# Value projection of a two-layer decoder trunk by seven block products instead of eight row-tile products, with the residual's affine moved

## The chip, the cores and the metric

The kernel runs on one core of one Trainium2 chip. A core has five engines that run side by side, each through its own queue in order: TensorE (PE in the profile; PEld is its weight load) multiplies matrices, VectorE (DVE) and ScalarE (ACT) work element by element, GpSimd (POOL) does small arithmetic and issues accumulating transfers, and SyncE (SP) issues plain transfers. Operands lie in SBUF with 128 partitions; matmul results land in the eight banks of PSUM, from which VectorE and ScalarE fetch them. The metric is device time in microseconds, the median of several executions. A profile is of one execution, and its span runs from the first to the last instruction.

## The reference

A sequence of 512 tokens with width 1024 passes two layers, all in float32. The first has gated linear attention, the second stick-breaking attention whose keys and values come from one shared projection of the first layer's output. Each layer ends with a squared-ReLU MLP, and after each half stands a residual sum with a layer norm.

```python
kv = h @ kv_w                      # (512, 1024) @ (1024, 2048): keys, then values
q = h @ sb_w_q[j]
o = stick_breaking_attention(q, k_sh, v_sh)
mix = o @ sb_w_o[j]
h = layer_norm(ALPHA * h + mix, ln_g[l, 0], ln_b[l, 0])
h = layer_norm(ALPHA * h + square(relu(h @ w_up)) @ w_down, ln_g[l, 1], ln_b[l, 1])
```

The change concerns the values, `h @ kv_w[:, 1024:]`, a product of 512 x 1024 by 1024 x 1024, and the affine (gain and bias) of the layer norm ahead of it.

## The kernel before

**Float32 by parts.** Each operand of a matmul is split into a high part (`hi`, rounded by a ScalarE copy) and a low part (`lo`, the rest, by a VectorE subtraction). A product is three matmuls, hi x hi, hi x lo and lo x hi (`mm3`, L91). Weights are split in tiles of 128 x 1024 (`split_tile`, L67), with three buffers of raw weights and six each of `hi` and `lo`. `put` (L97) splits anything else the same way.

**Seven products.** The MLP's second matrix is multiplied by Strassen's scheme in Winograd's form (`seven`, L294): tokens, inner dimension and columns are cut in halves, seven products of sums of blocks take the place of eight, and each product is 2 token tiles x 4 slices of 128 x 3 = 24 matmuls. The sums of weight blocks are made by accumulating transfers from GpSimd's queue (`more`) or by VectorE (L373, L383), in tiles tagged `B` with eight buffers. Columns of the second half come out negated, and adds become subtractions. Sums of activation blocks are VectorE operations on tiles of 128 x 1024, which `split_a` (L282) then splits.

**Around the change.** At the end of the first layer's MLP, `done0` (L743) calls `finish` (L245) with the steps that `seven` yields. For each 128-token tile: `stats` and `centre` (VectorE, with two small GpSimd operations between), then `turn`: for each half of the width, four TensorE transposes into a bank, four ScalarE operations that apply gain and bias (now one number per partition) into a scratch tile `y`, and `put` into the split transposed activations `h2T`. `y` is thrown away. Tiles 0 and 1 are turned within `seven`; tiles 2 and 3 come back as a list `late`.

Then (L767 to L773) the values are made plainly: for each half of the columns, four pairs of raw weight blocks are split, and for each token tile `rows` (L263) makes 24 matmuls of 512 columns into a bank, which ScalarE copies into `vs`. The two late turns stand behind the first two row tiles.

Attention follows in eight pairs of heads (L866 to L896). In step p: the key and query projections of pair p+2 with the transposes of pair p's weights between, scores and stick-breaking weights of pair p+1 (VectorE scans, L833, and products with them on GpSimd or, for the last, VectorE, L834), and outputs of pair p. In steps 1 to 4 the residual rows of one token tile get their gain and bias (`affine`, L192: four VectorE operations of 128 x 512).

**What sets the order.** The program's text is not the order of the queues. A planner simulates the engines and gives each engine, whenever it is free, the ready instruction that comes first in the program; `tc.high_priority()` raises some (the statistics and centring). So a later instruction that is ready fills a wait. `tc.keep_in_program_order` pins an instruction behind the one traced last on its engine. Buffers are handed out as they come free. The pool of the attention stage (`sb`) is opened when the MLP's has been closed, and takes its place in SBUF.

Of the kernel before, what the change touches and what calls it, by code (L numbers as in the profile page):

```python
# [8 lines left out]
F32 = mybir.dt.float32  # L9
F32R = mybir.dt.float32r  # L10
I32 = mybir.dt.int32
AF = mybir.ActivationFunctionType
# [22 lines left out]
def yoco_kernel(ctx: ExitStack, tc: tile.TileContext, x, gla_w_in, gla_w_a2, gla_b_a, gla_norm_g,  # L35
# [22 lines left out]
    def unit(dtype):  # L58
        return big.tile([P, 4, 512], dtype, tag="T", bufs=8, name=nm("T"))
# [166 lines left out]
    def turn_affine(sp, u, t, src, cols, y):  # L226

        g, b = cols
        ps = bank()
        for i in range(4):  # L230
            nc.tensor.transpose(out=ps[:, 128 * i:128 * i + 128], in_=src[:, 128 * i:128 * i + 128], identity=ident)  # L231
        for i in range(4):
            k, c = 4 * u + i, slice(128 * i, 128 * i + 128)
            nc.scalar.activation(y[:, c], ps[:, c], AF.Identity, bias=b[:, k:k + 1], scale=g[:, k:k + 1])
        c = slice(128 * t, 128 * t + 128)
        put(sp.hi[u][:, :, c], sp.lo[u][:, :, c], y.rearrange("p (a b) -> p a b", a=4))

    def by_tiles(mm):
        for t in range(NT):
# [2 lines left out]
            if t > 0:  # L242
                yield ~(t - 1)

    def finish(steps, cols, hs, sp, work):  # L245

        def turn(t, work):
            for u in range(2):  # L250
                turn_affine(sp, u, t, hs[t].h[:, 512 * u:512 * u + 512], cols, work())

        rest = list(range(NT))
        for t in steps:
            if t < 0:
                turn(~t, work)
                rest.remove(~t)
            else:
                hs[t].stats()
                hs[t].centre()  # L260
        return [lambda work, t=t: turn(t, work) for t in rest]
# [426 lines left out]
    def mlp(l, hT, late, vec, done):  # L688
# [45 lines left out]
        last, begun = up(NG - 1, lambda: ahead(sq[NG - 2]))  # L734
        sq.append(last)
        steps = down(NG - 2, begun=begun, norms=range(NT) if l == 0 else (2, 3), ends=True)
        got = done(steps, work)
        ml.__exit__(None, None, None)
        return got

    h2T = Split(0)

    def done0(steps, work):  # L743
        h2T.grow()
        h2T.grow()
        return finish(steps, lncols(0, 1), hs, h2T, work)

    late = mlp(0, hT, late, vec, done0)


    sbx = tc.tile_pool(name="sb", bufs=1, reuse_waits="tile")
# [11 lines left out]

    def chain():
        return sbp.tile([P, S], F32, tag="w", bufs=6, name=nm("w"))

    vs = [unit(F32), unit(F32)]  # L767
    for n in range(2):
        pcs = pieces_512(kv_w, 0, 8, D + 512 * n)
        for t in range(NT):  # L770
            nc.scalar.activation(vs[n][:, t, :], rows(h2T, t, pcs, K8), AF.Copy)
            if late:
                late.pop(0)(chain)  # L773

    HALVES = ((A0, A1), (A1, A0))

# [99 lines left out]
    for p in range(NP):  # L876
        if p + 2 < NP:
            pairs[p + 2].keys()
            made = pairs[p].turn()
            pairs[p + 2].queries(lambda k: [next(made, None) for _ in range(TAKE.get(k, 0))])  # L880
        else:
            n = p - (NP - 2)
            pcs = pieces_512(sb_w_o[0], 0, 4, 512 * n)
            made = pairs[p].turn()
            for t in range(NT):
                hs[t].add(n, rows(oA, t, pcs, range(4)), True)
                for _ in range(((0, 1, 2, 2), (1, 1, 2, 1))[n][t]):
                    next(made, None)
        if p + 1 < NP:
            pairs[p + 1].weights()  # L890
        if 1 <= p <= NT:
            hs[p - 1].affine(vec)
        if p in (4, 6):
            u = unit(F32R)
            parts += [(u[:, i, :], u[:, 2 + i, :]) for i in range(2)]
        pairs[p].outputs(*parts[p], LAST if p == NP - 1 else [(j, j, NT) for j in range(NT)])  # L896
# [13 lines left out]
    late = finish(by_tiles(part2), vcols, hs, h3T, chain)  # L910
    sbx.__exit__(None, None, None)

    def done1(steps, work):
        vec = lnvec(1, 1)


# [68 lines left out]
```

## Time and profile before

| | us |
|---|---|
| median of 3 runs (lowest to highest) | 1119.79 (1119.24 to 1119.84) |
| profiled execution, span | 1118.1 |
| median of the runs less this span | 1.7 |
| TensorE busy | 1110.7 |
| VectorE busy | 803.2 |
| ScalarE busy | 551.1 |
| GpSimd busy | 171.3 |

In the rows below, a number and L are a line of the kernel, `x` a count of instructions, an arrow goes from what is read to what is written, and a bracket at the end gives idle time ahead of an instruction and what ended it. In rows of the timeline the first number is the start in us from the span's start and the second the duration. Matmuls overlap in a pipeline, so their rate is read from starts or from long stretches, not from one row's duration.

### The profile page before, as it was taken

The numbers are of one execution on the slowest core, as the hardware profiler recorded it, in microseconds if no ns is written. First come the engines' busy times: TensorE is split into PE (matmuls) and PEld (weight loads), VectorE is DVE, ScalarE is ACT, GpSimd is POOL, SyncE is SP. The second block draws the span as 40 slices with busy tenths as digits, with TensorE's granted clock in tenths as the row PEclk, the third lists the DMA queues.
The fourth block names the chain that finished last, engine by engine and source line by source line (L and its number), as shares of the span: only waits on it lengthen the run. The fifth ranks groups of instructions, "written<-read, shape, count | busy, mean of one in ns | idle before, by whom it ended". The sixth has DMA issues, their size and how long they took to land.

```text
span 1118.1 us, 14353 instructions
## 1 busy us (share of the span) xinstructions
PE 1110.7 (99%) x5515; PEld 919.9 (82%) x5515; DVE 803.2 (72%) x967; ACT 551.1 (49%) x829; POOL 171.3 (15%) x213
## 2 busy tenths in 40 slices
PE   9999999999999999999999999999999999999997
PEld 7888888898888888888888778778988888888885
DVE  4677639958956856848945888887489767667677
ACT  4455437653533534535734666664445435336363
POOL 1011222200100100122200434330200000000232
PEclk9999999999999999999999999999999999999999
DMA  8441399492670770787344221212947816706783
GB/s 248 121 132 57 112 260 213 117 300 92 190 206 24 200 208 19 203 199 144 113 114 132 57 76 39 76 38 57 287 114 202 245 38 168 228 19 187 175 136 86
DMA packets 105368, 157.52 MB, mean 141 GB/s; under 512 B 12306, under 2 KB 37266, under 8 KB 105300
## 3 DMA queue, kind: packets, MB, share of 16 engines
q1 hardware_dynamic: 86772, 120.43, 33.4%
q0 software_dynamic: 18240, 35.66, 18.7%
q8 instruction: 43, 0.70, 0.2%
q10 hardware_dynamic: 288, 0.52, 0.1%
q14 instruction: 25, 0.20, 0.1%
HBM read 153.45 MB, written 3.15 MB: 140 GB/s over the span
## 4 chain that ended last, share of the span: by engine, by line
PE 98%; DVE 1%; issue 0%; POOL 0%; ACT 0%; POOLq 0%; DVEq 0%; ACTq 0%
PE ps L349 29%; PE ps L93 20%; PE ps L94 20%; PE ps L95 20%; PE ps L857 2%; PE ps L843 2%; PE ps L806 2%; PE ps L231 1%; PE ps L578 0%; DVE lo L72 0%; PE ps L121 0%; PE ps L643 0%; DVE bst L177 0%; DVE h L169 0%; PE ps L445 0%
## 5 line engine op out<-in xcount | busy, mean ns | idle before, releaser
L349 PE MATMUL ps<-hi,T 128*128 128x512 f32 x1008 | 313.2, 390 | 0.1
L93 PE MATMUL ps<-T,hi 128*128 128x512 f32 (+1 forms) x768 | 288.8, 376 | 0.0
L94 PE MATMUL ps<-T,hi 128*128 128x512 f32 (+1 forms) x768 | 285.6, 372 | 0.0
L95 PE MATMUL ps<-T,lo 128*128 128x512 f32 (+1 forms) x768 | 285.5, 372 | 0.0
L72 DVE TENSOR_TENSOR lo<-raw,hi 128x1024 fp32r<-128x1024 f32 x134 | 163.1, 1220 | 131.3 <-ACT hi L70 130.5
L70 ACT ACTIVATE hi<-raw 128x1024 fp32r<-128x1024 f32 x134 | 142.1, 1064 | 178.3 <-PE ps L94 62.4
L349 PEld LDWEIGHTS ps<-hi,T 128*128 128x128 f32 x1008 | 188.9, 188 | 40.0 <-DVE T L99 0.6
L349 PE MATMUL ps<-lo,T 128*128 128x512 f32 x504 | 196.1, 389 | 0.0
L70 ACT ACTIVATE hi<-B 128x1024 fp32r<-128x1024 f32 x108 | 114.1, 1059 | 159.2 <-PE ps L94 104.1
L72 DVE TENSOR_TENSOR lo<-B,hi 128x1024 fp32r<-128x1024 f32 x108 | 130.8, 1220 | 83.3 <-ACT hi L70 83.3
L95 PEld LDWEIGHTS ps<-T,lo 128*128 128x128 f32 x768 | 144.7, 188 | 25.1
L93 PEld LDWEIGHTS ps<-T,hi 128*128 128x128 f32 x768 | 144.7, 188 | 24.6 <-issue 0.9
L94 PEld LDWEIGHTS ps<-T,hi 128*128 128x128 f32 x768 | 144.8, 189 | 23.6
L308 POOL DMA_DIRECT2D B<-in_mlp_w_down_dram x52 | 62.8, 1244 | 542.8 <-DMA B<-in_mlp_w_down_dram 327.0
L349 PEld LDWEIGHTS ps<-lo,T 128*128 128x128 f32 x504 | 94.6, 188 | 19.6
L93 PE MATMUL ps<-hi,T 128*128 128x512 f32 x256 | 102.4, 400 | 0.0
L95 PE MATMUL ps<-hi,T 128*128 128x512 f32 x256 | 100.2, 392 | 0.0
L94 PE MATMUL ps<-lo,T 128*128 128x512 f32 x256 | 100.0, 391 | 0.0
L169 DVE TENSOR_TENSOR h<-h,ps 128x512 f32<-128x512 f32 x110 | 74.7, 680 | 6.9 <-PE ps L95 4.0
L834 POOL TENSOR_TENSOR w<-w,r 128x512 f32<-128x512 f32 x32 | 53.0, 1658 | 133.5 <-DVE r L833 125.7
L833 DVE TENSOR_TENSOR_SCAN r<-r,begin 128x512 f32<-128x512 f32 x40 | 66.2, 1659 | 2.4 <-ACT r L830 2.2
L95 PEld LDWEIGHTS ps<-hi,T 128*128 128x128 f32 x256 | 48.1, 188 | 10.9 <-DVE T L99 0.7
(179 smaller groups left out, 1161.2 us busy)
## 6 DMA issues: line engine op xcount, KB each, us to landing
raw<-in_mlp_w_up_dram SPq DMA_DIRECT2D x64, 512.0 KB, 5.5
B<-in_mlp_w_down_dram SPq DMA_DIRECT2D x64, 512.0 KB, 5.9
B<-in_mlp_w_down_dram POOLq DMA_DIRECT2D x52, 512.0 KB, 7.9
raw<-in_gla_w_in_dram SPq DMA_DIRECT2D x20, 512.0 KB, 3.7
raw<-in_mlp_w_down_dram SPq DMA_DIRECT2D x16, 512.0 KB, 4.4
raw<-in_kv_w_dram SPq DMA_DIRECT2D x16, 512.0 KB, 4.2
B<-in_gla_w_o_dram POOLq DMA_DIRECT2D x14, 512.0 KB, 7.8
B<-in_gla_w_o_dram SPq DMA_DIRECT2D x8, 512.0 KB, 7.7
```

Of the source, the lines that this page charges most:

```text
L70: nc.scalar.activation(hi, raw, AF.Copy)
L72: nc.vector.tensor_tensor(lo, raw, hi.bitcast(F32), op=ALU.subtract)
L93: keep(nc.tensor.matmul(ps, lhsT=a[0], rhs=b[0], start=first, stop=False))
L94: keep(nc.tensor.matmul(ps, lhsT=a[0], rhs=b[1], start=False, stop=False))
L95: keep(nc.tensor.matmul(ps, lhsT=a[1], rhs=b[0], start=False, stop=last))
L169: nc.vector.tensor_tensor(h, h, ps, op=op)
L308: nc.gpsimd.dma_start(out=b.rearrange("p (a b) -> p a b", a=2), in_=weights(k, h, j), accum_op=ALU.add)
L349: nc.tensor.matmul(banks[s], lhsT=a(k, s)[x], rhs=b[k][y], start=opens and (k, x, y) == (0, 0, 0), stop=closes and (k, x, y) == (3, 1, 0), ...
L806: nc.tensor.matmul(zs[b + a][:, at], lhsT=self.q[x][own, P * i:P * i + P], rhs=self.k[y][own, 0:n], start=(x + y == 0), stop=(x == 1), ski ...
L833: nc.vector.tensor_tensor_scan(down, down, begins[kind][:, ::-1], 1.0, op0=ALU.mult, op1=ALU.max)
L834: (nc.vector if kind == 2 else nc.gpsimd).tensor_tensor(w, w, r[:, 1:S + 1], op=ALU.mult)
L843: nc.tensor.transpose(out=ps[:, P * b:P * b + P], in_=w[:, P * b:P * b + P], identity=ident)
```

## The change

The values get a seven-product function of their own, `values`, which `done0` calls inside the MLP's pool. `finish` is handed a place for the turned rows: two tiles of the MLP's pool (`four()`) now keep the float32 `y` of all four token tiles, and the sums of activation blocks (a22, a21, a11, a12) are made from these. Three weight sums come about as follows: B22 + B12 and B12 + B11 by accumulating transfers (`more`), and two on VectorE, in two tiles each. B22 is loaded once more for the sixth product. The first two products (`ys`, `xs`) read `h2T` of the first token half alone, and the late turns stand behind the two token tiles of the first. The plain loop and its late turns go. In the attention steps `affine` is now given `tc.keep_in_program_order`.

```diff
@@ turn_affine
-            nc.scalar.activation(y[:, c], ps[:, c], AF.Identity, bias=b[:, k:k + 1], scale=g[:, k:k + 1])
+            nc.scalar.activation(y[:, i, :], ps[:, c], AF.Identity, bias=b[:, k:k + 1], scale=g[:, k:k + 1])
...
-        put(sp.hi[u][:, :, c], sp.lo[u][:, :, c], y.rearrange("p (a b) -> p a b", a=4))
+        put(sp.hi[u][:, :, c], sp.lo[u][:, :, c], y)
@@ finish
-    def finish(steps, cols, hs, sp, work):
+    def finish(steps, cols, hs, sp, work, room=None):
...
-                turn_affine(sp, u, t, hs[t].h[:, 512 * u:512 * u + 512], cols, work())
+                y = room(u, t) if room else work().rearrange("p (a b) -> p a b", a=4)
+                turn_affine(sp, u, t, hs[t].h[:, 512 * u:512 * u + 512], cols, y)
@@ mlp
-        got = done(steps, work)
+        got = done(steps, work, four, mlp_)
...
+    vs = []
+    def values(y, late, pool):
+        a11, a21, a12, a22 = y[0][:, :, 0:256], y[0][:, :, 256:512], y[1][:, :, 0:256], y[1][:, :, 256:512]
+        whole = lambda u, c0: lambda k, s: tuple(w[u][:, k, c0 + 128 * s:c0 + 128 * s + 128] for w in (h2T.hi, h2T.lo))
...
+        def load(k, j, more=None):
+            got = []
+            for h in range(2):
+                b = pool.tile([P, 1024], F32, tag="B", bufs=8, name=nm("B"))
+                v = b.rearrange("p (a b) -> p a b", a=2)
+                nc.sync.dma_start(out=v, in_=weights(k, h, j))
+                if more:
+                    nc.gpsimd.dma_start(out=v, in_=weights(*more(h)), accum_op=ALU.add)
+                got.append(b)
+            return got
...
+        def fresh(s, banks, i, j):
+            nc.scalar.activation(vs[j][:, 2 * i + s, :], banks[s], AF.Copy, scale=-1.0 if j else 1.0)
+        def add(s, banks, i, j):
+            v = vs[j][:, 2 * i + s, :]
+            tt(v, v, banks[s], op=ALU.subtract if j else ALU.add)
+        ys, xs, ws, zs = ([None, None] for _ in range(4))
+        b11, b21 = load(0, 0), load(1, 0)
+        b22 = load(1, 1, lambda h: (0, h, 1))
+        b12 = load(0, 1, lambda h: (0, h, 0))
+        p1, p2 = pieces(b11), pieces(b21)
+        for s in range(2):
+            part(s, whole(0, 0), p1, ys, True, False)
+            late.pop(0)(None)
+        for h in range(2):
+            tt(b11[h], b22[h], b11[h], op=ALU.add)
+            tt(b21[h], b21[h], b11[h], op=ALU.add)
+        p4 = pieces(b21)
+        vs.extend([unit(F32), unit(F32)])
+        for s in range(2):
+            part(s, whole(1, 0), p2, xs)
+        tt(a22, a22, a21, op=ALU.subtract)
+        p5 = split_a(a22), pieces(b12)
+        for s in range(2):
+            part(s, whole(1, 256), p4, ws)
+        for s in range(2):
+            fresh(s, ys, 0, 0)
+            add(s, xs, 0, 0)
+        tt(a21, a11, a21, op=ALU.subtract)
+        minus(a11, a22, a11)
+        p6 = split_a(a11), pieces(b11)
+        for s in range(2):
+            part(s, *p5, zs, True, False)
+            fresh(s, ws, 1, 0)
+            fresh(s, zs, 1, 1)
+        minus(a12, a12, a11)
+        p3 = split_a(a12), pieces(load(1, 1))
+        for s in range(2):
+            part(s, *p6, ys, False, False)
+            fresh(s, ys, 0, 1)
+        p7 = split_a(a21), pieces(b22)
+        for s in range(2):
+            part(s, *p3, zs, False, True)
+            add(s, zs, 0, 1)
+        for s in range(2):
+            part(s, *p7, ys, False, True)
+            add(s, ys, 1, 1)
+            add(s, ys, 1, 0)
...
-        return finish(steps, lncols(0, 1), hs, h2T, work)
+        y = [four(), four()]
+        late = finish(steps, lncols(0, 1), hs, h2T, work, lambda u, t: y[u][:, :, 128 * t:128 * t + 128])
+        values(y, late, pool)
...
-    vs = [unit(F32), unit(F32)]
-    for n in range(2):
-        pcs = pieces_512(kv_w, 0, 8, D + 512 * n)
-        for t in range(NT):
-            nc.scalar.activation(vs[n][:, t, :], rows(h2T, t, pcs, K8), AF.Copy)
-            if late:
-                late.pop(0)(chain)
...
-            hs[p - 1].affine(vec)
+            hs[p - 1].affine(vec, tc.keep_in_program_order)
```

`part` is the 12 matmuls of one token tile as in `seven`, and `pieces` splits a list of B tiles with `split_tile`. In the text the products are counted in the order in which they stand: `p1`, `p2`, `p4`, `p5`, `p6`, `p3`, `p7`.

More of the change, by code (lines that the diff above doesn't have):

```diff
@@ L741, in yoco_kernel, with pieces, part @@
     h2T = Split(0)
-    def done0(steps, work):
+    vs = []
+    def values(y, late, pool):
+        a11, a21, a12, a22 = y[0][:, :, 0:256], y[0][:, :, 256:512], y[1][:, :, 0:256], y[1][:, :, 256:512]
+        whole = lambda u, c0: lambda k, s: tuple(w[u][:, k, c0 + 128 * s:c0 + 128 * s + 128] for w in (h2T.hi, h2T.lo))
+        weights = lambda k, h, j: block(kv_w, 512 * k + 256 * h, D + 512 * j)
+        tt = nc.vector.tensor_tensor
+        def load(k, j, more=None):
[8 more added lines that the diff above has]
+            return got
+        def pieces(bs):
+            got = []
+            for b in bs:
+                hi, lo = split_tile(b, 2)
+                got += [(hi[:, i, :], lo[:, i, :]) for i in range(2)]
+            return got
+        def part(s, a, b, banks, opens=True, closes=True):
+            if opens:
+                banks[s] = bank()
+            for k in range(4):
+                for x, w in ((0, 0), (0, 1), (1, 0)):
+                    nc.tensor.matmul(banks[s], lhsT=a(k, s)[x], rhs=b[k][w],
+                                     start=opens and (k, x, w) == (0, 0, 0),
+                                     stop=closes and (k, x, w) == (3, 1, 0), skip_group_check=True)
+        def fresh(s, banks, i, j):
[26 more added lines that the diff above has]
+        tt(a21, a11, a21, op=ALU.subtract)
+        minus = lambda out, a, b: nc.vector.scalar_tensor_tensor(out, a, -1.0, b, op0=ALU.mult, op1=ALU.subtract)
+        minus(a11, a22, a11)
[17 more added lines that the diff above has]
+            add(s, ys, 1, 0)
@@ L744, in done0 @@
+    def done0(steps, work, four, pool):
         h2T.grow()
         h2T.grow()
-        return finish(steps, lncols(0, 1), hs, h2T, work)
-    late = mlp(0, hT, late, vec, done0)
+        y = [four(), four()]
+        late = finish(steps, lncols(0, 1), hs, h2T, work, lambda u, t: y[u][:, :, 128 * t:128 * t + 128])
+        values(y, late, pool)
+    mlp(0, hT, late, vec, done0)
     sbx = tc.tile_pool(name="sb", bufs=1, reuse_waits="tile")
@@ L911, in yoco_kernel, with done1 @@
     sbx.__exit__(None, None, None)
-    def done1(steps, work):
+    def done1(steps, work, *_):
         vec = lnvec(1, 1)
```

## The prediction

> **What bounds the kernel now.** I read the page's first and fourth parts, then windows around the stage that is changed, then single rows of each engine there.
>
> ```profile
> PE 1110.7 (99%) x5515; PEld 919.9 (82%) x5515; DVE 803.2 (72%) x967; ACT 551.1 (49%) x829; POOL 171.3 (15%) x213
> ...
> PE 98%; DVE 1%; issue 0%; POOL 0%; ACT 0%; POOLq 0%; DVEq 0%; ACTq 0%
> ```
>
> TensorE (PE) is busy 99% of the span and carries 98% of the chain that ended last. So time is won only where TensorE gets less to do, and only as long as the other engines keep it fed. The chain of waits, in order of time, gives its rate:
>
> ```profile
> 446.11 38.08 PE ps L349 x168
> ...
> 540.57 5.47 PE ps L349 x24
> ...
> 551.48 0.87 PE ps L231 x8
> ```
>
> An earlier pair of `down` groups, seven products of 24 matmuls, took 38.08 us for 168 matmuls: 0.2267 us each (the 0.39 us of a single row overlap). The MLP's last 24 end at 540.57 + 5.47 = 546.0, and there the value projection begins. A turn of one 128-token tile, eight transposes, is 0.87 us. The stage's last eviction:
>
> ```profile
> L771 ACT ACTIVATE T<-ps x8: 598/600/601, 551.5 to 591.4; 128x512 f32<-128x512 f32 x8
> ```
>
> It starts at 591.4. By the rates, 192 x 0.2267 + 2 x 0.87 = 45.3 us after 546.0 is 591.3: TensorE runs through the old stage without a gap. The windows show what room the others have:
>
> ```profile
> 506.00:546.00 40.00, 40.00 (x185) 32.97 (x184) 38.49 (x47) 25.31 (x38) 7.96 (x9) 1.00 0.56 120
> 546.00:559.00 13.00, 13.00 (x68) 10.87 (x67) 12.23 (x20) 8.88 (x18) 4.23 (x11) 1.00 0.51 158
> ...
> 576.00:588.00 12.00, 12.00 (x54) 9.95 (x53) 0.00 (x0) 1.90 (x3) 0.00 (x0) 1.00 0.16 46
> ```
>
> Columns are the stretch, its length, and busy time of PE, PEld, DVE, ACT and POOL, then granted clock (full), DMA share and GB/s. VectorE (DVE) is nearly full at the MLP's end (38.5 of 40 us, 12.2 of 13), and idle from 576 to 588. The change fills this idle stretch, but its first products must get through the full one.
>
> **The change part by part.** *Removed from TensorE:* 8 row tiles x 24 = 192 matmuls become 7 products x 24 = 168. 24 x 0.2267 = **-5.44 us**. The two turns stay. ScalarE's eight evictions stay too (now `fresh`).
>
> *Weights.* Eight splits of raw blocks become fourteen of B tiles. Ten plain loads go on SP in place of eight; four accumulating loads go on GpSimd's queue.
>
> ```profile
> B<-in_mlp_w_down_dram SPq DMA_DIRECT2D x64, 512.0 KB, 5.9
> B<-in_mlp_w_down_dram POOLq DMA_DIRECT2D x52, 512.0 KB, 7.9
> ...
> L308 POOL DMA_DIRECT2D B<-in_mlp_w_down_dram x52 | 62.8, 1244 | 542.8 <-DMA B<-in_mlp_w_down_dram 327.0
> ```
>
> The MLP's last B tiles are split in the 506 to 546 window, so slots come free from about 510 to 533; 5.9 + 7.9 us later, by about 547, the sums are there. I cost them at nothing, because VectorE has other work until then; uncovered, a sum that lands late moves the third product by as much. Each issue holds GpSimd 1.24 us, and the two `pow` of tiles 2 and 3 queue behind: 0 to 2 x 1.24 on a turn, which TensorE bridges with the other half of the first product, as that needs only tiles 0 and 1. 0 taken. The later raw loads of SP queue behind the tenth B load, which waits for a slot; their users start after 585, so 0.
>
> *Added to VectorE*, in the order in which it must come. These are its rows around the start:
>
> ```profile
> 545.52 0.68 DVE L169 TENSOR_TENSOR h<-h,ps 128x512 f32<-128x512 f32 x1
> 546.12 0.68 DVE L196 TENSOR_TENSOR h<-h,lng 128x512 f32<-128x512 f32 x1
> 546.72 0.68 DVE L177 BATCH_NORM_STATS2 bst<-h 128x6 f32<-128x512 f32 x1
> 547.33 0.67 DVE L99 TENSOR_TENSOR T<-s,T 128x512 fp32r<-128x512 f32 x1
> ...
> 548.59 1.21 DVE L72 TENSOR_TENSOR lo<-raw,hi 128x1024 fp32r<-128x1024 f32 x1
> 549.72 0.68 DVE L177 BATCH_NORM_STATS2 bst<-h 128x6 f32<-128x512 f32 x1
> 550.33 0.86 DVE L190 TENSOR_SCALAR h<-h,mv,rs 128x1024 f32<-128x1024 f32 x1
> ...
> 551.22 1.16 DVE L72 TENSOR_TENSOR lo<-raw,hi 128x1024 fp32r<-128x1024 f32 x1
> 553.15 0.81 DVE L190 TENSOR_SCALAR h<-h,mv,rs 128x1024 f32<-128x1024 f32 x1 [0.77 <-POOL rs L184]
> 553.88 1.22 DVE L72 TENSOR_TENSOR lo<-raw,hi 128x1024 fp32r<-128x1024 f32 x1
> ```
>
> From start to start a 128x1024 operation takes 1.13 (548.59 to 549.72) and a 128x512 one 0.60 (545.52 to 546.12). By 553.88 + 1.13 = 555.0 VectorE has done the adds, statistics and centring of tiles 2 and 3, the split at 548.59, one affine operation (546.12) and two more splits (551.22, 553.88), and was idle 0.77. In the new kernel the affine operation is gone and those two splits are not yet due: 0.60 + 2 x 1.13 + 0.77 = 3.6 us of room, which takes three of the four new 128x1024 weight sums. After 555.0 the **third product** (the one with the summed weights on the second token half) still needs: one sum 1.13, the low halves of both turns 4 x 0.60, its first weight split 1.13; together 4.7, so it can start at 559.7 at the earliest (its second split, 1.13, hides behind the 6 x 0.2267 = 1.36 us on the first). TensorE is there at 546.0 + 48 x 0.2267 + 2 x 0.87 = 558.6. The least stall is **1.1**.
>
> The most: VectorE takes what is ready, and the fourth product's weight splits (2 x 1.13) and the two adds of the second product (2 x 0.60) are ready before the chain of sum, ScalarE's copy and low half is; add one such copy for which VectorE waits:
>
> ```profile
> 484.37 2.00 ACT L70 ACTIVATE hi<-B 128x1024 fp32r<-128x1024 f32 x2
> ...
> 552.02 1.85 ACT L234 ACTIVATE w<-ps,bcol,gcol 128x128 f32<-128x128 f32 x5
> ```
>
> One copy is 2.00 / 2 = 1.0, so the most is 1.1 + 2.3 + 1.2 + 1.0 = 5.6. ScalarE is no easier just then: sixteen row-affine pieces at 1.85 / 5 = 0.37 lie ahead of that copy. The old rows show VectorE filling each short wait with whatever was ready (the affine piece at 546.12 between an add and its statistics), which is between the ends; I take **3.0**.
>
> *Fourth to seventh product.* From the third's start VectorE needs for the fourth a difference, its low half and two splits, 4 x 1.13 = 4.5, plus the third's second split 1.13: 5.7 against the 5.44 that the third lasts, with one ScalarE copy (1.0) inside the chain. 0 to 1.5; taken **0.6**. The sixth product's inputs cost 4.5 and the fifth's 5.7; the seventh's, with the two adds before it, 4.6, each against 5.44 of TensorE. Over the whole stage that is some 35 us of VectorE from 545.5 to 580, where TensorE starts the seventh at 580 plus the stalls: it fits, if hardly. Nothing more, bound 1. The last four adds fall into the key projection.
>
> *Residual's affine.* It leaves the value stage:
>
> ```profile
> L196 DVE TENSOR_TENSOR h<-h,lng 128x512 f32<-128x512 f32 x8 | 5.3, 685 | 0.0
> L196 DVE TENSOR_TENSOR h<-h,lnb 128x512 f32<-128x512 f32 x8 | 5.2, 685 | 0.0
> ```
>
> Sixteen operations at 0.60 are 9.6 us. All but the one counted above ran after 555; without the move they would only have filled leftover time, so it relieves nothing beyond that 0.60. Pinned behind the last VectorE operation of each pair's weights, they now come four at a time, 2.4 us, in pairs 1 to 4. A period of that stage:
>
> ```profile
> 665.16 1.23 DVE L72 TENSOR_TENSOR lo<-raw,hi 128x1024 fp32r<-128x1024 f32 x1 [2.44 <-ACT hi L70]
> ...
> 667.92 1.23 DVE L833 TENSOR_TENSOR_SCAN r<-r,begin 128x512 f32<-128x512 f32 x1 [0.20 <-ACT r L830]
> ...
> 669.37 2.12 DVE L833 TENSOR_TENSOR_SCAN r<-r,begin 128x512 f32<-128x512 f32 x1
> ...
> 676.87 1.30 DVE L834 TENSOR_TENSOR w<-w,r 128x512 f32<-128x512 f32 x1
> 678.10 0.68 DVE L99 TENSOR_TENSOR T<-ps,T 128x512 fp32r<-128x512 f32 x1
> 678.70 1.21 DVE L72 TENSOR_TENSOR lo<-raw,hi 128x1024 fp32r<-128x1024 f32 x1
> 679.83 0.68 DVE L99 TENSOR_TENSOR kl<-ps,kh 128x512 fp32r<-128x512 f32 x1
> 682.95 1.23 DVE L72 TENSOR_TENSOR lo<-raw,hi 128x1024 fp32r<-128x1024 f32 x1 [2.44 <-ACT hi L70]
> ```
>
> The period is 682.95 - 665.16 = 17.79, with 2.44 idle before the row at 682.95. The four go in at 678.10; the output's and the key's low halves and one split come 2.41 later, and the gap shrinks to 0.03. So **0**, with work on the path only past that gap: the whole of it uncovered is 4 x 2.41 = 9.6. Two PSUM banks (outputs, keys) are freed 2.4 later; the key's still at 683.0, when the next scores have just begun on other banks.
>
> The sum: -5.44 + 3.0 + 0.6 + 0 = -1.84. The profiled execution spans 1118.1, and the median of the runs is 1119.79, 1.7 around it. 1118.1 - 1.8 = 1116.3 of span, **1118.0** as a time. Its own range goes from -5.44 + 1.1 = -4.3 (1115.4) to -5.44 + 5.6 + 1.5 = +1.7 (1121.4).
>
> **The rivals.** *Full gain.* VectorE's order follows need: the third product waits 1.1 or less, nothing after. 1114.4 to 1115.6. For it: that order wants no more work than the rows show. Against: the rows fill each wait with what is ready, not with what is due.
>
> *Nothing left.* The change does not do what it says because VectorE becomes the bound: every low half comes late, the fourth and later products stall by some 0.5 each as well: -5.44 + 3.0 + 4 x 0.5 + a late sum of 1 is +0.6, 1120.4. For it: 12.23 of 13 us. Against: the idle 576 to 588, which the work can flow into.
>
> *Slower.* In pairs 1 to 4 the inserted operations outgrow the gap. It decides from 0.03 us per pair on, once the low halves of keys and outputs are late by more than scores and turns can wait. A scan beside GpSimd's product took 2.12 (669.37) where the first of a pair takes 1.23 (667.92), so an operation can stretch by 0.9 there; the gap lost in full gives 1118.0 + 9.6 = 1127.6, and four stretches a pair 14 us on top of what the gap hides, 1132. Against: they start at 678.10, when
>
> ```profile
> 675.84 1.79 POOL L834 TENSOR_TENSOR w<-w,r 128x512 f32<-128x512 f32 x1
> ```
>
> GpSimd's last product has ended, at 677.6. The Trainium skill, SBUF — State Buffer, section Who interferes with whom, says that a VectorE instruction with two inputs in SBUF blocks, or is blocked by, a GpSimd instruction that reads SBUF; the affine operations are of this kind, and the row at 669.37 agrees with it. By that rule they must stay behind 677.6, as the pin has them.
>
> **How the numbers follow.** Against no change a measurement here can tell about 0.2%, 2.24 us: faster is below 1117.55, slower above 1122.03. Forecast 0.62, full gain 0.14, nothing left 0.12, slower 0.12. Of the forecast's own range about two fifths lie below 1117.55: 0.14 + 0.26 = 0.40 faster; 0.12 slower and 0.01 for the forecast's upper end, 0.13; the rest, 0.47, the same. The range 1114.9 to 1121.5 leaves out the slower rival and the lowest part of the full gain, 0.05.
>
> **What would show it.** 168 matmuls on a new line at 0.2267; a TensorE gap of 1 to 5.6 us after 48 of them, released by a VectorE low half of a B tile, little or none later; affine operations behind 678 less the gain, with the idle 2.44 gone from four periods and the period still 17.8. Gaps in pairs 1 to 4, or none before the third product, would prove me wrong.

## The result and the profile after

The changed kernel takes **1127.79 us** (median, 1126.49 to 1130.47) against 1119.72 us (1119.24 to 1119.84) for the kernel before; the ratio is 1.0075, with a 95% interval of 1.006 to 1.0089. It is slower. The forecast was 1118.0 with a range up to 1121.5. The profiled execution took 1126.58 us and spans 1124.9, 6.8 more than the 1118.1 before. It is one of the two faster of the four runs, so the trace shows 6.8 of the 8.1 us between the medians; in the two slower runs the mean granted clock was 0.995 and 0.996, in the two faster 0.998.

The first part of the page after, and the group of the new matmuls from the view of groups by line, taken over the value stage alone:

```profile
PE 1109.5 (99%) x5491; PEld 917.6 (82%) x5491; DVE 828.1 (74%) x993; ACT 559.7 (50%) x839; POOL 176.2 (16%) x217
...
L777 PE MATMUL ps<-hi,T 128*128 128x512 f32 x112 | 35.6, 393 | 1.7 <-DVE T L99 1.0 <-ACT T L98 0.7
L777 PE MATMUL ps<-lo,T 128*128 128x512 f32 x56 | 22.0, 392 | 0.0
```

The 24 matmuls are gone (5515 to 5491), 168 stand on the new line, and VectorE has 24.9 us more to do. Three marks on TensorE cut the difference into stages: the first matmul of the values, the first scores and the last scores. Rows of the timeline, the kernel before:

```profile
545.88 0.39 PE L93 MATMUL ps<-hi,T 128*128 128x512 f32 x1
...
607.60 0.50 PE L806 MATMUL ps<-kh,qh 64*128 64x512 f32 x2
...
737.20 0.28 PE L806 MATMUL ps<-kh,ql 64*128 64x256 f32 x2
```

and the kernel after:

```profile
549.96 0.39 PE L777 MATMUL ps<-hi,T 128*128 128x512 f32 x1
...
611.68 0.50 PE L889 MATMUL ps<-kh,qh 64*128 64x512 f32 x2
...
743.50 0.28 PE L889 MATMUL ps<-kh,ql 64*128 64x256 f32 x2
```

| stage | before | after | difference |
|---|---|---|---|
| up to the first value matmul | 545.88 | 549.96 | +4.1 |
| from there to the first scores (values, then key and query of the first pairs) | 61.72 | 61.72 | 0.0 |
| first scores to last scores | 129.60 | 131.82 | +2.2 |
| from there to the end of the span | 380.9 | 381.4 | +0.5 |

So the value stage gained nothing from 24 fewer matmuls, and two neighbours became longer. What made the last 0.5 no run shows.

**Ahead of the values.** GpSimd's queue in the kernel after (L760 issues the accumulating loads of the value weights, L183 and L184 are `ve` and the `pow` of the statistics):

```profile
534.79 3.73 POOL L760 DMA_DIRECT2D B<-in_kv_w_dram  x3 [9.48 <-DVE h L169]
538.07 0.90 POOL L183 TENSOR_SCALAR ve<-mv 128x1 f32<-128x1 f32 x2
540.33 1.22 POOL L760 DMA_DIRECT2D B<-in_kv_w_dram  x1 [1.36 <-DMA B<-in_kv_w_dram]
541.10 1.94 POOL L184 TENSOR_TENSOR rs<-ve,mhalf 128x1 f32<-128x1 f32 x2
```

The same tiles' statistics before:

```profile
535.91 0.22 POOL L183 TENSOR_SCALAR ve<-mv 128x1 f32<-128x1 f32 x1 [13.64 <-DVE mv L182]
536.21 0.57 POOL L184 TENSOR_TENSOR rs<-ve,mhalf 128x1 f32<-128x1 f32 x1
```

The `pow` of tiles 0 and 1 stands behind the fourth accumulating load, which waits until 540.33 for its own plain load to land: 4.9 us late (541.10 against 536.21). The chain of waits of the kernel after, in order of time, shows that this lay on the path (columns: start, length, what):

```profile
531.88 1.07 ACT hi L70
...
534.23 5.54 DMA B<-in_kv_w_dram
539.84 0.49 issue
540.33 1.22 POOL B L760
541.55 0.62 POOL rs L184
542.20 0.82 DVE h L190
543.07 3.35 PE ps L231 x16
...
558.19 0.82 DVE h L190
559.06 1.09 PE ps L231 x8
```

TensorE waits 2.27 us before the turns at 543.07 and then needs 3.35 us for sixteen transposes, where 2 x 0.87 = 1.74 was the old price. The window after this wait:

```profile
543.00:546.00 3.00, 2.93 (x16) 2.93 (x17) 2.94 (x5) 2.10 (x6) 0.04 (x1) 0.58 1.12 204
```

The granted clock was 0.58 there. The chain also shows that the load which `pow` queued behind started only at 534.23, when VectorE had split the MLP's late weight (531.88) and its buffer was free.

At 559.06 a second wait of 2.47 us stands before tile 3's turn, again behind `pow` and centring. Two more follow in the fifth product, at 577.55 and 579.74. From start to start, less 0.2267 for the matmul between, the three cost 2.6, 0.9 and 1.2 us, 4.7 together. The rest is spread out: the last 68 matmuls take 15.70 us from 579.74, 0.231 each in place of 0.2267, which over 168 is 0.7. That makes the 5.4 us that the seven products saved.

**In the pairs.** VectorE in the kernel after, between two scores, and TensorE beside it:

```profile
664.43 1.28 DVE L196 TENSOR_TENSOR h<-h,lng 128x512 f32<-128x512 f32 x2
665.63 1.28 DVE L196 TENSOR_TENSOR h<-h,lnb 128x512 f32<-128x512 f32 x2
666.84 0.68 DVE L99 TENSOR_TENSOR T<-ps,T 128x512 fp32r<-128x512 f32 x1
667.44 1.21 DVE L72 TENSOR_TENSOR lo<-raw,hi 128x1024 fp32r<-128x1024 f32 x1
668.57 0.68 DVE L99 TENSOR_TENSOR kl<-ps,kh 128x512 fp32r<-128x512 f32 x1
...
669.31 0.50 PE L889 MATMUL ps<-kh,qh 64*128 64x512 f32 x1 [0.52 <-DVE kl L99]
```

The scores wait for the key's low half, which the four affine operations pushed back. This happens in two of the four pairs, whose periods are 18.84 and 18.83 us (from 668.29 to 687.13 and from 704.96 to 723.79) where 17.79 was usual.

### The profile page after: what moved, and what is told of

It reads as the page before. It is cut to its first block, busy times and chain, and to the rows that moved or that the text cites. A ratio compares the mean times of both kernels' runs of the same rounds, so it can differ in the third digit from the quotient of the medians.

```text
span 1124.9 us, 14368 instructions
## 1 busy us (share of the span) xinstructions
PE 1109.5 (99%) x5491; PEld 917.6 (82%) x5491; DVE 828.1 (74%) x993; ACT 559.7 (50%) x839; POOL 176.2 (16%) x217
## 4 chain that ended last, share of the span: by engine, by line
PE 88%; DVE 3%; issue 3%; DMA 3%; POOL 1%; ACT 0%; POOLq 0%; DVEq 0%; ACTq 0%
PE ps L350 23%; PE ps L93 18%; PE ps L94 18%; PE ps L95 18%; PE ps L777 3%; DMA B<-in_mlp_w_down_dram 2%; PE ps L940 2%; PE ps L889 2%; PE ps L926 1%; PE ps L231 1%; DVE lo L72 1%; DVE T L99 1%; POOL B L309 1%; DMA B<-in_kv_w_dram 0%; DVE h L169 0%
## 5 line engine op out<-in xcount | busy, mean ns | idle before, releaser
L350 PE MATMUL ps<-hi,T 128*128 128x512 f32 x1008 | 313.6, 390 | 0.1
L72 DVE TENSOR_TENSOR lo<-raw,hi 128x1024 fp32r<-128x1024 f32 x126 | 153.6, 1222 | 105.9 <-ACT hi L70 105.6
L350 PEld LDWEIGHTS ps<-hi,T 128*128 128x128 f32 x1008 | 189.3, 188 | 40.1 <-DVE T L99 0.6
L70 ACT ACTIVATE hi<-raw 128x1024 fp32r<-128x1024 f32 x126 | 133.4, 1062 | 165.7 <-PE ps L94 65.4
L70 ACT ACTIVATE hi<-B 128x1024 fp32r<-128x1024 f32 x122 | 128.4, 1061 | 173.3 <-PE ps L94 105.4
L72 DVE TENSOR_TENSOR lo<-B,hi 128x1024 fp32r<-128x1024 f32 x122 | 147.9, 1222 | 88.1 <-ACT hi L70 88.1
L350 PE MATMUL ps<-lo,T 128*128 128x512 f32 x504 | 196.2, 389 | 0.0
L93 PE MATMUL ps<-hi,T 128*128 128x512 f32 x192 | 77.5, 404 | 0.0
L95 PE MATMUL ps<-hi,T 128*128 128x512 f32 x192 | 75.3, 392 | 0.0
L94 PE MATMUL ps<-lo,T 128*128 128x512 f32 x192 | 75.0, 391 | 0.0
L99 DVE TENSOR_TENSOR T<-s,T 128x1024 fp32r<-128x1024 f32 (+1 forms) x50 | 53.5, 1071 | 6.9 <-ACT T L98 6.9
```

The source lines that it names most:

```text
L70: nc.scalar.activation(hi, raw, AF.Copy)
L72: nc.vector.tensor_tensor(lo, raw, hi.bitcast(F32), op=ALU.subtract)
L93: keep(nc.tensor.matmul(ps, lhsT=a[0], rhs=b[0], start=first, stop=False))
L94: keep(nc.tensor.matmul(ps, lhsT=a[0], rhs=b[1], start=False, stop=False))
L95: keep(nc.tensor.matmul(ps, lhsT=a[1], rhs=b[0], start=False, stop=last))
L99: keep(nc.vector.tensor_tensor(lo, ps, hi.bitcast(F32), op=ALU.subtract))
```

## The experiments

All are compared with runs of the kernel before on the same chip (median 1119.6 to 1120.2). The ratio has an interval of its own and isn't the quotient of two medians: for e10 that would be 1.0020. The three marks are read from the rows as above, and are those of one execution of each kernel; the times of one kernel lie 2.0 (e2) to 8.9 us (e14) apart. A difference of some tenths between two marks shows little by itself.

| run | median us | ratio, 95% interval | first value matmul | first scores | last scores |
|---|---|---|---|---|---|
| before | 1119.7 | | 545.88 | 607.60 | 737.20 |
| after | 1127.79 | 1.0075, 1.006 to 1.0089 | 549.96 | 611.68 | 743.50 |
| e1_pin_only | 1122.76 | 1.0024, 1.0014 to 1.0034 | 545.99 | 608.92 | 740.66 |
| e2_no_pin | 1127.33 | 1.0066, 1.0051 to 1.0081 | 550.14 | 614.89 | 744.69 |
| e4_early_affine | 1125.29 | 1.0047, 1.003 to 1.0065 | 547.70 | 610.12 | 740.74 |
| e7_spread_pin | 1121.11 | 1.0017, 1.0007 to 1.0026 | 545.22 | 608.14 | 737.74 |
| e3_pow_first | 1122.93 | 1.0027, 1.0015 to 1.0039 | 548.07 | 607.90 | 739.70 |
| e5_loads_held | 1122.24 | 1.0025, 1.0015 to 1.0035 | 545.83 | 607.61 | 739.43 |
| e6_turn_order | 1124.89 | 1.0048, 1.0033 to 1.0063 | 544.86 | 609.93 | 741.75 |
| e8_all | 1123.05 | 1.0034, 1.0022 to 1.0045 | 545.81 | 609.40 | 739.20 |
| e10_best | 1122.15 | 1.0014, 1.0004 to 1.0025 | 545.35 | 607.86 | 737.66 |
| e9_no_sums | 1118.86 | 0.9991, 0.9981 to 1.0002 | 545.82 | 604.89 | 734.69 |
| e11_gpsimd_sums | 1128.96 | 1.0082, 1.0068 to 1.0097 | 546.17 | 615.01 | 744.88 |
| e12_sums_behind | 1121.20 | 1.0003, 0.9993 to 1.0013 | 545.47 | 607.49 | 737.29 |
| e13_sums_turns | 1121.92 | 1.0015, 1.0006 to 1.0024 | 546.05 | 608.50 | 738.30 |
| e14_sums_unheld | 1123.03 | 1.0024, 1.0008 to 1.004 | 549.93 | 611.47 | 741.27 |

### The affine alone, and the change without it

```diff
 e1: the kernel before with
-            hs[p - 1].affine(vec)
+            hs[p - 1].affine(vec, tc.keep_in_program_order)
 e2: the changed kernel without this line
```

> The kernel before, with only the affine of steps 1 to 4 pinned behind the pair's weights. Theory A (in the changed kernel two of the four insertions make the scores wait some 1.05 us each for a key's low half, and this comes from the pin alone): 1119.7 + 2.1 to 2.7 = 1121.8 to 1122.4, with TensorE waits ahead of the scores in the pair stage and the value stage as it was. Theory B (the pair stage is slower only because the value stage hands over its work late): 1119.7 within 0.7, no such waits. My prediction's step (the gap of 2.44 takes it all) is B's number too.

> The changed kernel with the affine of steps 1 to 4 left to the planner, as before the change. Theory A: the pair stage gives back 2.1 to 2.7, and the sixteen operations (9.6 us of VectorE) fill waits in the value stage; if VectorE only waits there for others, the sum is 1124 to 1125; if VectorE is what the value stage waits for, up to 9.6 come on top and the time is 1128 to 1134. Theory B (pair stage not from the pin): no gain in the pair stage, 1126.5 or more.

In e1 the time from first to last scores is 131.74 against 129.60, with the same two waits on TensorE; the row of one of them:

```profile
666.50 0.50 PE L806 MATMUL ps<-kh,qh 64*128 64x512 f32 x1 [0.55 <-DVE kl L99]
```

In e2 that time is back to 129.80. So the pin costs 2.1 to 2.2 us in the pairs whether the seven products are there or not. e2's time of 1127.33 lies between the two that theory A allows, and theory B's reason, no gain in the pairs, is not what happened. Its value stage grows from 61.72 to 64.75, with waits of 2.44 and 2.09 us at 559.26 and 580.40. This isn't shown to be the affine's work: only two of the sixteen operations stand between the waits (1.28 us at 563.20) and the others come from 592 on, behind both. What e2 has there and the changed kernel has not is TensorE's clock at 0.50 to 0.51 behind both waits, from 560.5 to 563.5 and from 580.5 to 584. The 19 matmuls from 560.11 and from 580.40 take 7.71 us in place of 19 x 0.2267 = 4.31, so the low clock alone is worth some 3.4 us, an estimate from these starts.

### Where the affine costs nothing

```diff
 e4: the changed kernel, four operations behind each of these
     pairs[0].keys()
+    hs[0].affine(vec, pin)
     pairs[0].queries()
+    hs[1].affine(vec, pin)
...
 e7: the kernel before, four behind pairs[0].keys(), then in steps 0 to 5
-        if 1 <= p <= NT:
-            hs[p - 1].affine(vec)
+        if p < 6:
+            for op in spare[2 * p:2 * p + 2]:
+                op()
```

> The changed kernel with the sixteen affine operations pinned in fours behind the first key, query and key projections and the first pair's weights, where VectorE has waits of 3 to 4.7 us each, in place of steps 1 to 4. Theory A: the waits of the scores in steps 1 to 4 go, 2.1 to 2.7 less than the changed kernel on the same chip, 1124. If VectorE's sum of work over the attention stage were the limit, wherever it stands: no change, 1126.5 or more.

> The kernel before, with the same sixteen pinned affine operations as e1, four of them behind the first key projection and the other twelve two per step in steps 0 to 5, 1.2 us each time in place of 2.4. Theory F (the cover of a pinned operation was the 1.4 us between the end of the key's low half, 680.5, and the start of the scores that need its bank, 681.9, and not the 2.44 us gap behind it): no waits ahead of the scores, 1120.2 on this chip within 0.7, against e1's 2.6 more. Rival (VectorE's total in the pair stage): the same 2 us as in e1, for the same 9.6 us of work.

e4 takes about half of the pairs' loss away (130.62, one wait of 0.31 left), and its operations now stand ahead of the first scores. In e7, with two operations a step, the pairs take 129.60 as before, and no row of TensorE waits for `kl`. So the loss comes from four operations, 2.41 us, standing in one place; two, 1.20, pass. As a whole e7 is still slower (1.0017): its value stage is 1.2 longer (62.92), as is e1's (62.93), and both have a wait of 0.67 for a weight's low half there, which the kernel before has not. In both the order was planned anew with the affine out of that stage.

### GpSimd's queue and the transfers

```diff
 e3: the changed kernel, accumulates queued behind tile 1's pow
-                    nc.gpsimd.dma_start(out=v, in_=weights(*more(h)), accum_op=ALU.add)
+                    with tc.issue_after(hs[1].powed):
+                        nc.gpsimd.dma_start(out=v, in_=weights(*more(h)), accum_op=ALU.add)
 e5: e3, and the value loads held until the MLP's last accumulate has landed
-                nc.sync.dma_start(out=v, in_=weights(k, h, j))
+                ld = nc.sync.dma_start(out=v, in_=weights(k, h, j))
+                tc.add_manual_dep(ld.ins, accs[-1].ins.name, ...)
```

> The changed kernel with the four accumulating loads of the value weights queued behind the second normalised tile's power operation on GpSimd. Theory A (the fourth of them, waiting for its plain load, held the power operations of tiles 0 and 1 for 4 us; TensorE idled 2.3 us and then ran 3.5 us at a clock of about 0.58): the first value matmul starts at 546 in place of 550 and 4.1 us are gone, 1122.5; the sums land up to 3 us later and may give up to 3 of it back. Theory C (VectorE was late by itself, by its load at the end of the MLP): the turns of tiles 0 and 1 stay at 543 and the time at 1126.5 or more.

> The changed kernel with the accumulating loads behind the second tile's power operation, as in e3, and all ten plain loads of value weights held until the MLP's last accumulating load has landed. Theory D (in the changed kernel the first value loads run beside the MLP's last chain of accumulating loads and make it land some 4 us late, so that the last weight split of the MLP, and with it the turns of tiles 0 and 1, come late even in e3, where TensorE still waits 1.9 us): the split returns from 533 to 528, the first value matmul from 548.1 to 546, 2 us less than e3, 1120.5 to 1121. The other side: the weight sums land later, at 550 or after, and the third product waits up to 3 us for them. Rival E (the order on VectorE's queue is what makes those turns late): first value matmul stays at 548, the time at that of e3, 1122.9.

e3 starts the values at 548.07, 1.9 earlier than the changed kernel; e5 at 545.83, where the kernel before had them, and all later versions that hold the loads start between 544.86 and 546.17. So the 4.1 us have two causes, but the marks don't give the size of each. Of e3's 1.9 us some 1.6 are the low clock (3.35 against 1.74 for sixteen transposes), which followed the changed kernel's wait of 2.27 and not e3's of 1.89. e4, which leaves GpSimd's order as it was, starts at 547.70 at full clock, and e14, which has e3's order, at 549.93 with the clock fallen. The second cause is the early loads themselves. The MLP's last accumulating loads, in GpSimd's queue before:

```profile
512.03 1.20 POOL L308 DMA_DIRECT2D B<-in_mlp_w_down_dram  x1 [3.75 <-DMA B<-in_mlp_w_down_dram]
514.78 1.20 POOL L308 DMA_DIRECT2D B<-in_mlp_w_down_dram  x1 [1.55 <-DMA B<-in_mlp_w_down_dram]
521.06 1.20 POOL L308 DMA_DIRECT2D B<-in_mlp_w_down_dram  x1 [5.08 <-DMA B<-in_mlp_w_down_dram]
```

and after:

```profile
512.10 1.20 POOL L309 DMA_DIRECT2D B<-in_mlp_w_down_dram  x1 [3.67 <-DMA B<-in_mlp_w_down_dram]
517.19 1.20 POOL L309 DMA_DIRECT2D B<-in_mlp_w_down_dram  x1 [3.89 <-DMA B<-in_mlp_w_down_dram]
524.11 1.20 POOL L309 DMA_DIRECT2D B<-in_mlp_w_down_dram  x1 [5.71 <-DMA B<-in_mlp_w_down_dram]
```

Each waits for its plain load; with the value loads in flight beside them (DMA share 1.06 instead of 0.69 from 516 to 524) the last goes out 3.05 us later, and ScalarE gets the MLP's last weights at 531.88 instead of 527.98. In e5 the share from 516 to 524 is 0.65 again. Yet e5's first scores, at 607.61, are no earlier than those of the kernel before, and only 0.3 earlier than e3's; the ratios of e3 and e5, 1.0027 and 1.0025, don't differ. What e5 wins ahead of the values it loses in them: its value stage takes 61.8 against e3's 59.8, with one wait of 3.31 us before tile 2's turn and a clock of 0.53 behind it. So the loads held cost about what they win. e3 with the affine spread as in e7 was not run.

### What holds the value stage

```diff
 e6: e5, tile 2's turn behind both halves of the first product,
     tile 3's between the halves of the second
 e8: e6 with the affine spread as in e7
 e10: e5 with the affine spread as in e7
 e9: e10 with the four sums left out
-            tt(b11[h], b22[h], b11[h], op=ALU.add)
-            tt(b21[h], b21[h], b11[h], op=ALU.add)
 e11: e10 with these four as nc.gpsimd.tensor_tensor
 e12: e10 with these four inside
+        with tc.issue_after(hs[3].centred):
 e13: e12 with the turns of e6
 e14: e12 with the loads not held
```

> e5 with the two late turns moved in the program: tile 2's behind both halves of the first product, tile 3's between the halves of the second. If TensorE's waits ahead of the two turns (1.5 and 0.7 us in e3, 0.3 and 2.5 in the changed kernel) come from the order written there, they go, 1.5 to 2.5 us less than e5; if the next product's inputs are what is late, the wait only moves to the third product and the time stays within 0.7 of e5.

> The seven products with all of it: accumulating loads behind the power operation, plain loads held, turns reordered as in e6, affine spread as in e7. By the theories: e6 less 2.2, 1117 to 1118.5, below the kernel before; what VectorE's load leaves of the 5.44 us is read from it. If the value stage is bound by VectorE whatever the order, 1119 to 1120.

> The changed kernel with the value loads held behind the MLP's last accumulate, GpSimd's accumulates behind tile 1's pow, the turns where the planner puts them, and the residual's affine spread two operations a step. If the terms found so far add up: the held loads gave 1122.2 with 131.5 us from the first to the last scores; spread out, that stage takes 129.4, so 1122.2 - 2.1 = 1120.1, within 0.5 of the kernel before, with first scores at 607.6. If the terms do not add (the affine's operations ahead of the scores push the stage), above 1121.5.

> The changed kernel with the value loads held behind the MLP's last accumulate, GpSimd's accumulates behind tile 1's pow and the residual's affine spread two operations a step, and with the four VectorE sums of the value weights (b11 = b22 - ... and b21 + b11, 128x1024 each) left out: its output is not the reference's. It is compared with the run of the same kernel with the sums in it. Theory V (VectorE's load bounds the value stage: 20.0 of 20 us busy from 566 to 586): 4 x 1.13 = 4.5 us less on VectorE bring the first scores 3.5 to 4.5 us earlier than 607.6, to 603.1 to 604.1, and the time to 1116 to 1117.5. Theory L (the stage is held by the latency of the chains adds, statistics, GpSimd's pow, centring and by the order of the turns, and VectorE is full only because it catches up): the waits of TensorE at tile 2's turn stay, the first scores come less than 1.5 us earlier, time 1118.5 to 1120.

> As the kernel with held loads and spread affine, but the four sums of the value weights are made by GpSimd. From GpSimd's 1.79 us for a 128x512 product, 3.6 us each, 14 us for the four, behind the two pow of tiles 2 and 3. Theory V (VectorE's load bounds the stage): VectorE loses 4.5 us of work; the third product's operand is there 14 us after the sums' loads land (about 546 to 548), at 561 or so, 2 to 3 us late, and later products gain: first scores 605 to 607, time 1118 to 1119.5. Theory P (VectorE's two-input operations stretch beside GpSimd's, or the sums hold tile 2's pow): first scores at 608 to 611, time 1120.5 to 1123, with VectorE rows over 1.5 us beside the GpSimd sums.

The change makes four weight sums, not three: two by accumulating transfers and two on VectorE, these in two tiles each. The four here are VectorE's operations. e9 leaves them out, so its values are not the reference's; it serves for its time alone.

e6 and e8 cut the wait at tile 2's turn to 1.52 and to nothing that the rows show, and TensorE then waits within the third and fourth products instead (1.54, 0.61, 0.83 and 1.07 in e6; 1.52, 0.61 and 0.60 in e8). Both came out slower than any of their expectations, and e6 (1.0048) slower than e5 (1.0025), whose turns it moves. e10 shows why tile 2 is late at all. VectorE, and below it TensorE, in e10:

```profile
544.99 0.68 DVE L169 TENSOR_TENSOR h<-h,ps 128x512 f32<-128x512 f32 x1
547.86 1.23 DVE L801 TENSOR_TENSOR B<-B,B 128x1024 f32<-128x1024 f32 x1 [2.19 <-DMA B<-in_kv_w_dram]
549.00 0.69 DVE L177 BATCH_NORM_STATS2 bst<-h 128x6 f32<-128x512 f32 x1
...
551.40 0.81 DVE L190 TENSOR_SCALAR h<-h,mv,rs 128x1024 f32<-128x1024 f32 x1 [0.45 <-POOL rs L184]
...
552.27 1.97 PE L231 MATMUL ps<-ident,h 128*128 128x128 f32 x8 [4.04 <-DVE h L190]
```

The first weight sum (L801) stands in VectorE's queue between tile 2's last add and its statistics and waits 2.19 us for its transfer; the statistics start at 549.00, 3.16 later than in e12 (545.84), where no sum stands ahead of them, and TensorE waits 4.04. e9, which has none of the four sums, waits 1.07 there and reaches the scores 2.97 us earlier than e10, between what its two theories had said. That fits two causes, this place in the queue or 4 x 1.13 = 4.5 us less for VectorE to do, so e12 and e13 kept all the work and changed the place, and e14 left the loads free again.

> The changed kernel with held loads, GpSimd's accumulates behind tile 1's pow, spread affine, and the four weight sums ordered behind tile 3's centring on VectorE; all the work is kept. Theory O (it was the order: a sum that waits for a DMA stood ahead of tile 2's statistics): tile 2 is centred at 549 to 550 as in the kernel without sums, TensorE waits 1 there instead of 4.04, later 1 to 2 at the third product, first scores at 605 to 606.5 against 607.86, time 1118 to 1119.5. Theory V (it was VectorE's capacity): the waits at tile 2 go down but come back before the third to fifth products, first scores at 607.3 or later, time 1120.5 to 1122.

> As the kernel with the sums behind tile 3's centring, with tile 2's turn put behind both halves of the first product and tile 3's between the halves of the second. Theory O: TensorE has 2.7 us more of work ahead of tile 2's turn, which covers the last 1 us of wait there; the third product's operands are later, so 1 to 2 us of wait there; first scores at 605 to 607, time 1118 to 1120, within 1 of the kernel with the planner's turns. Theory V: as for that kernel, 607.3 or later.

> As the kernel with the sums behind tile 3's centring, but the value loads not held behind the MLP's last accumulate: they run beside it, as in the changed kernel. The MLP's last weights then come about 3 us late as they did with loads not held (first value matmul 548.1 against 545.8), but the sums' operands land earlier. Theory O with contention as found: first scores 2 us later than with held loads, 607 to 608.5, time 1120 to 1121.5. If the contention costs nothing by itself, within 0.5 of the kernel with held loads.

Two rows of TensorE's timeline in e12, the stretch up to the second wait and the one behind it:

```profile
549.43 1.09 PE L231 MATMUL ps<-ident,h 128*128 128x128 f32 x8 [1.07 <-DVE h L190]
...
573.06 0.80 PE L781 MATMUL ps<-hi,T 128*128 128x512 f32 x1 [2.09 <-ACT T L98]
...
552.00:573.00 21.00, 18.97 (x86) 14.90 (x84) 20.88 (x22) 19.54 (x32) 0.00 (x0) 1.00 0.42 88
573.00:576.50 3.50, 3.44 (x8) 2.77 (x9) 3.46 (x4) 1.92 (x4) 0.00 (x0) 0.52 0.00 0
```

The wait at tile 2's turn goes from 4.04 to 1.07, as in e9, and comes back as 2.09 before the fifth product, with a low clock behind it; the first scores are at 607.49, 0.4 earlier than in e10 and 2.6 later than in e9. These are theory V's numbers, but not its mechanism alone. From 552 to 573 VectorE is busy 20.88 of 21 us, but ScalarE is nearly as full (19.54), and the 2.09 us are in the larger part ScalarE's. The chain of waits of e12, then a row of VectorE and one of ScalarE:

```profile
554.18 16.80 PE ps L781 x72
...
571.00 1.06 ACT hi L70
572.06 0.95 ACT T L98
...
569.42 1.22 DVE L816 SCALAR_TENSOR_TENSOR s<-s,s 128x1024 f32<-128x1024 f32 x1
...
571.00 1.06 ACT L70 ACTIVATE hi<-B 128x1024 fp32r<-128x1024 f32 x1 [0.30 <-PE ps L781]
```

TensorE is through with the fourth product at 570.98. The sum of activations that the fifth needs leaves VectorE at 569.42 + 1.22 = 570.64. But in ScalarE's queue the copy of a weight tile (L70), which itself waits for TensorE, stands ahead of the copy of that sum (L98). ScalarE was through with the copy before at 569.64 + 1.06 = 570.70, and L98 takes 1.0. With L98 first TensorE could have gone on at about 571.7 and not at 573.06. By this estimate 0.7 us of the wait are VectorE's lateness and 1.3 the place in ScalarE's queue. Then come nine matmuls from 573.06 to 576.76, 3.70 us in place of 9 x 0.2267 = 2.04, so the low clock adds 1.7. The changed kernel, e2 and e14 have such a copy ahead of L98 there too. In e2 the sum left VectorE at 575.29 + 1.22 = 576.5, and its copy began at 579.31, behind two weight copies that had waited for TensorE (1.59 and 0.30). In e10, with all of VectorE's work, L98 stands first and TensorE does not wait before the fifth product; but TensorE is later there as a whole.

So e9 against e12 shows that without the 4.5 us of sums the first scores come 2.6 us earlier, and that the sums' place alone doesn't give this back in the traces. How much of the 2.6 is VectorE's load and how much ScalarE's order and the clock stays open: no run moved that copy. Over all runs the place counts for more than the marks say: the ratios of e10, e12 and e9 are 1.0014, 1.0003 and 0.9991, about equal steps, and the interval of e12 overlaps both others.

e13 moves the turns and is 1.0 later at the first scores. e14 does not hold the loads and starts the values 4.5 us later than e12 (a wait of 2.39 before the turns of tile 0, then a low clock); its ratio is 1.0024 against 1.0003, with intervals that just overlap. Here holding the loads seems to pay, where e3 and e5 showed no difference.

e12 is the best version that does all the work, and it ends level with the kernel before (1.0003, 0.9993 to 1.0013); none was faster. e11, slower than either of its theories had it, shows that GpSimd can't take the sums as they stand. GpSimd's queue, then VectorE:

```profile
549.50 2.33 POOL L801 TENSOR_TENSOR B<-B,B 128x1024 f32<-128x1024 f32 x1 [1.75 <-DMA B<-in_kv_w_dram]
...
557.19 0.57 POOL L184 TENSOR_TENSOR rs<-ve,mhalf 128x1 f32<-128x1 f32 x1
...
560.51 2.38 POOL L802 TENSOR_TENSOR B<-B,B 128x1024 f32<-128x1024 f32 x1
...
560.58 2.86 DVE L190 TENSOR_SCALAR h<-h,mv,rs 128x1024 f32<-128x1024 f32 x1 [0.77 <-POOL rs L184]
```

Three sums went ahead of tile 2's `pow`, which came at 557.19, and TensorE waited 9.61 us. The sums were cheaper than expected (2.33 against 3.6). Behind `pow` they would not block it; that was not run.

## Why the prediction was wrong, by its steps

The forecast was -1.8 for the span and the trace has +6.8, 8.6 apart: 4.1 ahead of the values, 1.8 in them (5.4 lost where the sum had 3.0 + 0.6), 2.2 in the pairs and 0.5 behind the last scores.

- **-5.44 for 24 matmuls: right.** 168 rows stand on the new line. The value stage took as long as before with 5.4 us of losses in it.
- **"I cost them at nothing" (the weights' loads) and the two `pow` ("0 taken"): wrong, +4.1 us.** The step looked at the `pow` of tiles 2 and 3, and at 1.24 us an issue. It was those of tiles 0 and 1 that queued behind the issues, and what they waited for was not the issue's own time but the plain load that the fourth accumulate waits for (1.36 idle on GpSimd's queue, `pow` 4.9 us late). For tiles 0 and 1 no other half product was there to bridge. The loads were costed only by when they land, not by what they slow down: the MLP's last accumulate went out 3.05 us later. e3 and e5 show both causes; of the 4.1 some 1.6 are the low clock behind the wait, which the sum had no term for.
- **"TensorE bridges with the other half of the first product": wrong.** The planner put tile 3's turn ahead of the second product, and TensorE waited 2.47 us there with all of that product still to come. e6 gave it the bridge, and waits came back in the third and fourth products.
- **Third product 3.0 (1.1 to 5.6), later ones 0.6: the size of the sum was low, its place wrong.** The losses are 2.6 at tile 3's turn, 0.9 and 1.2 in the fifth product and 0.7 spread out, 5.4 in all; the sum had 3.6. No gap stands before the third product, which the prediction named as a sign that it is wrong. "It fits, if hardly" and "nothing more, bound 1" is the step that broke for the later products. VectorE is busy without a break from 566 to 586, as these rows of the window view show, before and then after. ScalarE goes from 5.64 to 16.12 of 20 us in the same stretch, and the prediction allowed its queue one copy of 1.0 at the third product and one at the fourth:

```profile
566.00:586.00 20.00, 20.00 (x90) 16.54 (x89) 5.45 (x5) 5.64 (x8) 0.00 (x0) 1.00 0.51 158
```

```profile
566.00:586.00 20.00, 18.27 (x79) 14.15 (x78) 20.00 (x19) 16.12 (x21) 0.00 (x0) 1.00 0.15 54
```

- **The affine, "so 0": wrong, +2.2 us.** Its 2.41 us were held against the idle 2.44 behind the key's low half. But the scores need that low half. It ended at 679.83 + 0.68 = 680.5 in the rows of before, and this row of TensorE before has the next scores:

```profile
681.91 0.50 PE L806 MATMUL ps<-kh,qh 64*128 64x512 f32 x2
```

  The cover was 681.9 - 680.5 = 1.4 us, not 2.44, and 2.41 - 1.4 = 1.0 is what two pairs lost each (1.05 and 1.04). Why the other two of the four lost nothing was not worked out. e7's two operations, 1.20, fit under the cover. The idle time was on the wrong side of the operation that mattered.
- **The rival "nothing left"** (VectorE becomes the bound) has the size of the value stage, which gained nothing; that VectorE alone was the bound is not shown, as said under e12. Its 1120.4 lacked the neighbours' losses of 4.1 and 2.2. The rival **"slower"** had the right place, the pairs, and a size (9.6) that four pairs fully uncovered would have; two paid 1.05 and 1.04. Its stretching beside GpSimd's products did not happen in the pairs: the affine rows at 664.43 and 665.63 are two operations in 1.20 us each, behind GpSimd's last product, which ended at 662.17 + 1.79 = 663.96.

## What to carry to other kernels

Cover is measured from the end of the operation that is pushed back to whoever waits for it, not by the idle time on the engine that does the pushing. An accumulating load that waits for its own plain load holds what stands behind it in GpSimd's queue, so look which small operations of the critical path queue there. Loads that are issued early run beside other transfers; ask which chain they lengthen. Trading TensorE's matmuls for sums needs slack on the other engines in that very stage, ScalarE's copies too: here 5.44 us of matmuls stood against 24.9 us more of VectorE, and the best order that was tried came out even. When a wait is put down to one engine's load, read the chain: the order of another engine's queue may hold the larger part.

## What the runs showed of the hardware that was not expected

**TensorE's clock falls after short waits.** A wait of 2.27 us (543.07, changed kernel) was followed by 3 us at a granted clock of 0.58, and one of 2.09 us (573.06, e12) by 3.5 us at 0.52, matmuls starting 0.43 apart instead of 0.2267. The same shows behind nine of the other ten waits of over 2 us: 2.39 and 2.09 (e14), 2.47, 2.44 and 2.09 (e2), 2.44 (e4), 3.31 (e5), 4.04 (e10) and 9.61 us (e11), and not behind the 2.47 us at 559.06 in the changed kernel. No single wait of 1.89 us or less was followed by it, but two close together were in e13 (1.55 at 563.78 and 0.61 at 565.13, then 0.52 from 565 to 568.5) and in e8 (1.52 and 0.61, then 0.51 from 567 to 570.5), and not in e6 (1.54 and 0.61). So a wait of some 2 us can cost about 1.6 us more than its length (16 transposes in 3.35 instead of 1.74), and whether it does can't be told from its length alone. The Trainium skill, TensorE: Matmul & The Clock Gate, section "HAM oscillation — how this bites in real kernels", sets the limit at idle gaps over some 3.4 us; the rows here show the half clock after 2.1 to 2.5 us, and the measurement decides.

**VectorE stood still beside a GpSimd sum.** The centring at 560.58 in e11 took 2.86 us, where 0.81 is usual. It began just behind a GpSimd sum (560.51, 2.38 long) and ended at 563.44, 0.55 after it. The Trainium skill, SBUF — State Buffer, section Who interferes with whom, says that the two engines share a pair of ports which one of them can hold for a whole instruction; this row agrees.
